# A decoder trunk on one core: a second tile for the queries' low parts, raw output weights in alternating halves of the queries' tile, and three rotating tiles for the heads' outputs

## Chip, core and metric

The kernel runs on one core of one Trainium2 chip. The metric is the device time of one launch in microseconds (us), the median of three runs. Engines are named as in the profile: PE (matrix products, with PEld for the loading of their stationary operand), DVE (elementwise and reductions), ACT (activations and copies), POOL, and SP, whose queue issues most DMAs. Each engine takes its own instructions in the order in which they stand in its queue.

## What is computed

Two layers over 512 tokens of width 1024. Each layer has a mixer (differential attention, a short convolution and gated linear attention, concatenated to width 1024 and projected by `w_out`) and then a PEER block with 16384 single-neuron experts. Cut to the part around the change:

```python
for i in range(2):
    h = rmsnorm(x, norm_mix[i])
    da_q, da_k, da_v, sc_b, sc_c, sc_h, g_q, g_k, g_v, g_r, g_lr = split(h @ w_in[i])
    q, k = rope(da_q), rope(da_k)                    # 4 heads, 2 maps of 64 each
    p = softmax(causal(q @ k.T / 8))                 # for both maps
    o_da = rmsnorm((p[0] - lam * p[1]) @ v) * (1 - lam_init)
    o_sc = sc_b * conv3(sc_c * sc_h)                 # 256 channels
    o_g = rmsnorm(gla(g_q, g_k, g_v, decay)) * silu(g_r)
    x = x + concat(o_da, o_sc, o_g) @ w_out[i]       # 1024 x 1024
    x = x + peer(rmsnorm(x), ...)                    # top-16 of 16384 experts per head
return rmsnorm(x)
```

## The kernel before

Tokens are handled in four blocks of 128 (`tb` 0 to 3). To keep float32 precision on the faster matmul format, an operand is kept as two tiles: `hi`, a rounded copy made by ACT, and `lo`, the difference, made by DVE (`split`, lines 88 to 90). A product is then three matmuls (`mm3`, lines 82 to 86).

**The order of the work.** The program is written as one straight sequence, but a scheduler at build time lays each engine's queue out by readiness, with the program's order as priority, except where `keep_in_program_order` pins an instruction. So work of a later line can stand earlier in a queue, as filler. Tiles are slots of pools: a tile that takes over a slot waits until the last reader of the tile before it is done. Pools are stacked, so a pool that opens after another has closed lies in its space.

**The projections.** `across` and `down` (lines 277 to 295) load 256 columns of `w_in` at a time as a slab, split them and multiply with the normed activations. The result group (`psp`) is gathered in one of two PSUM tiles of `psC`.

**The attention.** The queries stand transposed in `qT`, 128 partitions by 4 heads by 512 tokens, 8 KB in each partition. For a block, `turn_hi` (line 391) makes the tile `qz` with four ACT copies of 64 partitions by 512 elements; `turn_lo` (line 397) makes `ql`, the low part, with two DVE subtractions. There are two tiles `qz0` and `qz1`, taken in turn by the blocks, but one tile `ql` for all blocks, cleared once by POOL (line 388). `attend(tb)` (line 401) goes through `diff_attention` and, per head, `head_weights`: scores on PE (lines 525 to 528), maxima on DVE (529), exponentials on ACT (533), the difference of the two maps on DVE (537), then transposes (553) and products with the values on PE (557). `head_norm` (from line 564) squares on ACT and takes a reciprocal root on DVE by some ten small operations. Blocks 0 and 1 are attended among the convolution's projections; two heads of block 2 are prepared early, at line 432; the rest of block 2 and block 3 follow at line 479, and `turn_lo(3)` stands just ahead of block 3, at line 477, since it can't overwrite `ql` while block 2 reads it.

**The output weights.** `w_out` is eight chunks of 128 rows, taken in the order 6, 7, 4, 5, 0, 1, 2, 3. `load_w` (line 441) fetches one chunk (512 KB) by a DMA from SP's queue into the first half of `qT`, tokens 0 to 255 of each head, whose queries are no longer needed by then; ACT and DVE split it into a tile `wk` of its own. All eight chunks go through this one place, so each fetch waits for the subtraction of the chunk before it. The first three tiles `wk` lie in the keys' tile `kT` and in the pool `early`; the other five in the pool `wout`, which opens when the slabs' pool has closed.

**The output projection.** `head_out` (line 576) transposes a block's heads' outputs and writes them, scaled by `dgain`, to `mh` and `ml`, two tiles for all four blocks. `out_proj(tb)` (line 464) forms two groups (`pso`, 512 columns each) of eight chunks, 24 matmuls a group; DVE adds each to `x`. In the program all four blocks' `head_out` stand ahead of the first `out_proj`. `norm_T` then normalizes block after block for PEER. The last group of block 3 and its addition come in `rest`, pinned among PEER's first instructions: the loads of its query weights into `uraw` (line 781), their splits (784, 785) and the products `psq`.

Of the kernel before, what the change touches and what calls it, by code (L numbers as in the profile page):

```python
# [7 lines left out]
F32 = mybir.dt.float32  # L8
F32R = mybir.dt.float32r
# [5 lines left out]
OP = mybir.AluOpType  # L15
# [4 lines left out]
P = 128  # L20
T = 512
# [51 lines left out]
class K:  # L73
# [156 lines left out]
    def mixer(self, L):  # L230
        nc, tc, ins = self.nc, self.tc, self.ins
        lam_init = 0.8 - 0.6 * math.exp(-0.3 * L)
        right = ExitStack()
        with ExitStack() as mc:
            mp = mc.enter_context(tc.tile_pool(name="mix", bufs=1, reuse_waits="tile"))
            dgain = mp.tile([P, 1], F32, name="dgain")
            cw = mp.tile([P, 2, 3], F32, name="cw")
            qT = mp.tile([P, 4, T], F32, name="qT")
            kT = mp.tile([P, 4, T], F32, name="kT")
            va = mp.tile([P, TB, T], F32, name="va")  # L240
# [6 lines left out]
            with ExitStack() as wc:  # L247
# [29 lines left out]
                def across(c0, n=256):  # L277
                    wh, wl = slab(c0, n)
                    for j in range(n // P):
                        ps = self.psC.tile([P, T], F32, tag="c", name="psp")  # L280
                        for k in range(KD):
                            self.mm3(ps, wh[:, k, j * P:j * P + P], wl[:, k, j * P:j * P + P], hh[:, k], hl[:, k],
                                     k == 0, k == KD - 1)
                        yield j, ps
# [15 lines left out]
                for i, tb in enumerate(ORDER):  # L300
                    if L:
                        ps = self.psv.pop(tb)
                    else:
                        next(norm, None)
                        ps = self.psC.tile([P, 256], F32, tag="c", name="psv")
# [18 lines left out]
                lam = mp.tile([P, 1], F32, name="lam")  # L324
# [4 lines left out]
                for tb in range(TB):  # L329
                    ps = self.psC.tile([P, 272], F32, tag="c", name="psp")  # L330
# [24 lines left out]
                for i in range(4):  # L355
                    dst, h = (qT, kT)[i // 2], i % 2
# [17 lines left out]
                ap = right.enter_context(tc.tile_pool(name="attn", bufs=2, side="right", reuse_waits="tile"))  # L374
                ac = mc.enter_context(ExitStack())
                kp = ac.enter_context(tc.tile_pool(name="early", bufs=1, side="right", reuse_waits="tile"))
                new_w = lambda pool, bufs: pool.tile([P, 2, D], F32R, tag="wk", name="wk", bufs=bufs)
                wk = [new_w(kp, 2) for _ in range(2)]
                kp.tile([P, 40], F32, name="line")
                keys = [kp.tile([P, 4, T], F32R, name=f"ks{m}") for m in range(2)]  # L380
                halves = [slice(64 * m, 64 * m + 64) for m in range(2)]
                for m, r in enumerate(halves):
                    for i in range(0, 4, 2):
                        h = slice(i, i + 2)
                        nc.scalar.copy(keys[m][r, h], kT[r, h])
                        nc.vector.tensor_tensor(keys[m][halves[1 - m], h], kT[r, h], keys[m][r, h].bitcast(F32), op=OP.subtract)
                ql = ap.tile([P, 4, 2, P], F32R, name="ql", bufs=1)
                nc.gpsimd.memset(ql.bitcast(F32), 0.0)
                heads, turned = [], {}

                def turn_hi(tb):
                    qz = turned[tb] = ap.tile([P, 4, 2, P], F32R, tag=f"qz{tb % 2}", name=f"qz{tb % 2}", bufs=1)
                    for m, r in enumerate(halves):
                        for half in halves:
                            nc.scalar.copy(qz[half, :, m], qT[r, :, tb * P:tb * P + P])

                def turn_lo(tb):
                    for m, r in enumerate(halves):
                        nc.vector.tensor_tensor(ql[r, :, m], qT[r, :, tb * P:tb * P + P], turned[tb][r, :, m].bitcast(F32), op=OP.subtract)

                def attend(tb, early=()):
                    heads.append(self.diff_attention(tb, keys, va, (turned[tb], ql), lam, ap, early))

                turn_hi(0)
                turn_lo(0)
                turn_hi(1)
                attend(0)
                z = qp.tile([P, 2, T + 2], F32, tag="z", name="z", bufs=1)
                nc.vector.memset(z[:, :, 0:2], 0.0)
                for j, ps in across(2048):  # L410
                    nc.scalar.copy(z[:, j, 2:], ps)
                turn_lo(1)
                attend(1)
                turn_hi(2)
                turn_lo(2)
                turn_hi(3)
                for j, ps in across(1792):
                    nc.vector.tensor_tensor(z[:, j, 2:], ps, z[:, j, 2:], op=OP.mult)
                nc.sync.dma_start(cw, ins["conv_w"][L])
# [9 lines left out]
                for j, ps in across(1536):  # L429
                    if j == 0:  # L430
                        s0 = self.sums()
                        early = [s0] + [self.head_weights(2, h, keys, (turned[2], ql), lam, ap, s0) for h in range(2)]
                    nc.vector.tensor_tensor(ys[j], ys[j], ps, op=OP.mult)
                    self.split(mch[:, j], mcl[:, j], ys[j])

                korder = (6, 7, 4, 5, 0, 1, 2, 3)
                wo = {}

                by4 = lambda t: t.rearrange("p (a b) -> p a b", a=4)

                def load_w(k, tile, raw):
                    wo[k] = tile
                    nc.sync.dma_start(raw, by4(ins["w_out"][L, k * P:(k + 1) * P, :]))
                    self.split(by4(tile[:, 0]), by4(tile[:, 1]), raw)

                for k, t in zip(korder, [mp.tile([P, 2, D], F32R, tag="kT", name="wk0")] + wk):
                    load_w(k, t, qT[:, :, 0:256])

            with tc.tile_pool(name="wout", bufs=1, reuse_waits="tile") as op_:
                mh = op_.tile([P, 4, T], F32R, name="mh")  # L450
                ml = op_.tile([P, 4, T], F32R, name="ml")
                for k in korder[3:]:
                    load_w(k, new_w(op_, 5), qT[:, :, 0:256])

                def chunk(k, s):
                    if k < 4:
                        return mh[:, k, s], ml[:, k, s]
                    a, b = (mch, mcl) if k < 6 else (mgh, mgl)
                    return a[:, k % 2, s], b[:, k % 2, s]

                def add(xs, ps):
                    return nc.vector.tensor_tensor(xs, xs, ps, op=OP.add)

                def out_proj(tb):
                    for nh in range(2):
                        ps = self.psC.tile([P, T], F32, tag="c", name="pso")
                        n = slice(nh * 512, nh * 512 + 512)
                        for k in korder:
                            self.mm3(ps, *chunk(k, slice(tb * P, tb * P + P)), wo[k][:, 0, n], wo[k][:, 1, n],
                                     k == korder[0], k == korder[-1])  # L470
                        if nh == 0 or tb < TB - 1:
                            add(self.x[:, tb, n], ps)
                    return self.x[:, tb, n], ps

                for tb in range(TB):
                    if tb == 3:
                        turn_lo(3)
                    if tb > 1:
                        attend(tb, early if tb == 2 else ())
                    t = slice(tb * P, tb * P + P)  # L480
                    self.head_out(heads[tb], dgain, mh[:, 0:4, t], ml[:, 0:4, t])
                xh, xl = self.new_act()
                norm = self.norm_T(ins["norm_ffn"][L:L + 1, :], xh, xl,
                                   [ap.tile([P, D], F32, tag=t, name=n, bufs=b) for n, t, b in
                                    (("grow", "qz0", 1), ("sq", "qz1", 1), ("xn0", "e", 2), ("xn1", "e", 2))], self.rs3, rows=self.xrows)
                for tb in range(TB):
                    late = out_proj(tb)
                    if tb < TB - 1:
                        next(norm)

# [927 lines left out]
```

## Time and profile before

| | |
|---|---|
| median of 3 runs | 2873.4 us (2873.01 to 2874.69) |
| the profiled execution, its own time | 2872.77 us |
| its span, first to last instruction | 2870.7 us |
| mean granted PE clock over the span | 0.998 |
| busy over the span | PE 99%, PEld 88%, DVE 86%, ACT 45%, POOL 29% |
| HBM traffic over the span | 273 GB/s |
| output projection of layer 0, first `pso` to first `psq` | 196.2 to 266.4 us |
| output projection of layer 1 | 1619.2 to 1690.0 us |

The profile's times run from the span's start. A line of a timeline gives start, duration, engine, source line, operation, output and inputs, count, and in square brackets how long the engine stood idle before it and whose end released it. A matmul's record is longer than the distance to the next one, because they are pipelined. In tables by stretches of time, each engine's busy microseconds and number of instructions are followed by the mean granted PE clock and the DMA engines' share. SPq is SP's queue, a DMA's issue and not its transfer.

### The profile page before, as it was taken

Reading aid. Unit: us, or ns where it says so; the run is one execution under the profiler, and the core shown is the slowest. Engines: PE = TensorE matmul, PEld = TensorE weight load, DVE = VectorE, ACT = ScalarE, POOL = GpSimd, SP = SyncE. Lnnn points to the kernel's source line nnn. Section 1 sums busy time; section 2 is a strip of 40 time slices with the busy share of each in tenths; the row PEclk is TensorE's granted clock in tenths of the full one; section 3 lists DMA queues with packets and bytes.
Section 4 is the critical chain, followed back from the end, with each engine's and each line's share of the span. In section 5 each row is a group of like instructions: output and inputs, shape, how many; then the busy total and the mean of one; then the engine's idle time right before and its main releaser. Section 6 shows DMA issues by size and latency. Waiting matters only on the chain.

```text
span 2870.7 us, 44994 instructions
## 1 busy us (share of the span) xinstructions
PE 2835.3 (99%) x16328; PEld 2528.3 (88%) x16328; DVE 2468.4 (86%) x4898; ACT 1290.8 (45%) x1946; POOL 840.0 (29%) x713
## 2 busy tenths in 40 slices
PE   8999999999999999999999999999999999999998
PEld 7878899999999988888888788999999999988887
DVE  6685989997998899888966869999979888998888
ACT  6273346675333333333453633556743333333333
POOL 1200002211666565222112000121126655552221
PEclk9999999999999999999999999999999999999999
DMA  4322259998999999999733222699989999999995
GB/s 133 96 71 92 89 164 318 331 307 308 375 383 376 381 377 363 369 359 363 270 99 89 74 85 91 210 314 325 317 303 384 386 379 386 375 363 366 364 357 222
DMA packets 352191, 790.50 MB, mean 275 GB/s; under 512 B 32384, under 2 KB 201248, under 8 KB 347872
## 3 DMA queue, kind: packets, MB, share of 16 engines
q1 hardware_dynamic: 165616, 424.18, 41.1%
q0 software_dynamic: 87136, 312.85, 29.8%
q10 hardware_dynamic: 99216, 50.60, 5.9%
q8 instruction: 128, 2.10, 0.3%
q14 instruction: 95, 0.78, 0.1%
HBM read 705.39 MB, written 78.91 MB: 273 GB/s over the span
## 4 chain that ended last, share of the span: by engine, by line
PE 85%; DVE 9%; ACT 2%; DMA 2%; issue 1%; SPq 0%; DVEq 0%; ACTq 0%
PE pv L85 12%; PE pv L86 12%; PE pv L84 12%; PE psh L84 10%; PE psh L85 10%; PE psh L86 10%; PE psg L1347 2%; PE psq L84 2%; PE psq L85 2%; PE psq L86 2%; PE psp L85 2%; PE psp L86 2%; PE psp L84 2%; DMA qT<-in_w_out 1%; PE pss L819 1%
## 5 line engine op out<-in xcount | busy, mean ns | idle before, releaser
L86 PE MATMUL pv<-vh,wl 128*128 128x512 f32 x1500 | 584.7, 390 | 0.0
L85 PE MATMUL pv<-vl,wh 128*128 128x512 f32 x1500 | 584.6, 390 | 0.0
L84 PE MATMUL pv<-vh,wh 128*128 128x512 f32 x1500 | 583.6, 389 | 0.0
L883 POOL DMA_INDIRECT row<-in_u_rows,idx x256 | 360.2, 1407 | 343.0 <-DVE row L889 225.1
L883 POOL DMA_INDIRECT row<-in_v_rows,idx x256 | 315.6, 1233 | 487.4 <-DVE yacc L896 450.1
L1049 DVE TENSOR_TENSOR vl<-vraw,vh 128x1024 fp32r<-128x1024 f32 x250 | 305.9, 1224 | 91.5 <-issue 79.1
L889 DVE SCALAR_TENSOR_TENSOR row<-row,xg 128x1024 f32<-128x1024 f32 x320 | 382.2, 1218 | 0.1
L1053 ACT CAST vh<-vraw 128x1024 fp32r<-128x1024 f32 x250 | 263.0, 1052 | 194.1 <-PE pv L86 188.0
L1061 ACT CAST wh<-g 128x384 fp32r<-128x384 f32 x250 | 128.4, 513 | 468.1 <-DVE g L1217 458.5
L84 PE MATMUL psh<-ahi,uwb 128*128 128x352 f32 x1024 | 334.1, 326 | 0.0
L84 PE MATMUL psh<-ahi,uwa 128*128 128x352 f32 x1024 | 333.6, 326 | 0.0
L86 PEld LDWEIGHTS pv<-vh,wl 128*128 128x128 f32 x1500 | 281.5, 188 | 58.8
L84 PEld LDWEIGHTS pv<-vh,wh 128*128 128x128 f32 x1500 | 281.6, 188 | 57.5
L85 PEld LDWEIGHTS pv<-vl,wh 128*128 128x128 f32 x1500 | 281.5, 188 | 57.2
L85 PE MATMUL psh<-alo,uwb 128*128 128x352 f32 x1024 | 330.6, 323 | 0.0
L85 PE MATMUL psh<-alo,uwa 128*128 128x352 f32 x1024 | 330.6, 323 | 0.0
L86 PE MATMUL psh<-ahi,uwa 128*128 128x352 f32 x1024 | 327.3, 320 | 0.0
L896 DVE SCALAR_TENSOR_TENSOR yacc<-row,wk,yacc 128x1024 f32<-128x1024 f32 x254 | 325.1, 1280 | 2.0
L86 PE MATMUL psh<-ahi,uwb 128*128 128x352 f32 x1024 | 326.8, 319 | 0.0
L800 ACT ACTIVATE ht<-psh 128x352 f32<-128x352 f32 x256 | 118.9, 465 | 458.7 <-PE psh L86 449.2
L785 DVE TENSOR_TENSOR uwa<-uraw,uwa 128x1024 fp32r<-128x1024 f32 x144 | 175.7, 1222 | 74.2 <-ACT uwa L784 74.0
L785 DVE TENSOR_TENSOR uwb<-uraw,uwb 128x1024 fp32r<-128x1024 f32 x144 | 175.9, 1221 | 57.9 <-ACT uwb L784 57.7
(389 smaller groups left out, 5822.2 us busy)
## 6 DMA issues: line engine op xcount, KB each, us to landing
uraw<-in_peer_u SPq DMA_DIRECT2D x256, 512.0 KB, 5.9
vraw<-in_v_rows SPq DMA_DIRECT2D x252, 512.0 KB, 7.4
G<-stg ACTq DMA_DIRECT2D x48, 1024.0 KB, 7.2
g<-G SPq DMA_DIRECT2D x30, 1536.0 KB, 10.4
H<-ht SPq DMA_DIRECT2D x144, 176.0 KB, 5.3
ht<-H SPq DMA_DIRECT2D x144, 176.0 KB, 8.5
wraw<-in_w_in SPq DMA_DIRECT2D x84, 256.0 KB, 3.2
uraw<-in_peer_w_q SPq DMA_DIRECT2D x32, 512.0 KB, 3.6
```

Source lines behind the costliest of these rows:

```text
L84: mm(ps, ah, bh, start=first, stop=False)
L85: mm(ps, ah, bl, start=False, stop=False)
L86: return mm(ps, al, bh, start=False, stop=last)
L785: self.before, self.last = self.last, pin(nc.vector.tensor_tensor(lo, src, hi.bitcast(F32), op=OP.subtract))
L800: pin(nc.scalar.activation(hs[c][:, 0:TD], ps, AF.Gelu))
L883: nc.gpsimd.indirect_dma_start(out=r, out_offset=None, in_=ins[name], in_offset=bass.IndirectOffsetOnAxis(ap=at, axis=0))
L889: nc.vector.scalar_tensor_tensor(r, r, 1.0, xg, op0=OP.mult, op1=OP.mult, accum_out=out)
L896: nc.vector.scalar_tensor_tensor(acc, r, w, acc, op0=OP.mult, op1=OP.add)
L1049: return pin(nc.vector.tensor_tensor(like(lo, src), src, like(hi.bitcast(F32), src), op=OP.subtract))
L1053: pin(nc.scalar.copy(vh[c], vs[c]))
L1061: pin(nc.scalar.copy(like(wh[c], ws[c]), ws[c]))
L1347: nc.tensor.matmul(ps[:, j], B[at], a[at], start=a is As[0], stop=a is As[-1])
```

## The change

- Two tiles `ql0` and `ql1`, both cleared by POOL at the start; block `tb` uses `ql[tb % 2]`. `turned[tb]` now holds both tiles of a block.
- `turn_lo(1)` moves ahead of `attend(0)`; `turn_lo(3)` moves from the output projection's loop to just behind `turn_hi(3)`, after `attend(1)`.
- `load_w` fetches into the first half of `qT` (tokens 0 to 255) and the second half (256 to 511) in turn.
- `mh` and `ml` (8 KB each in a partition) go. Each block gets a tile `m` of 4 KB for both parts, one of three that rotate; block 3 therefore takes the slot of block 0, and `head_out(3)` moves behind `out_proj(0)`.

```diff
-ql = ap.tile([P, 4, 2, P], F32R, name="ql", bufs=1)
-nc.gpsimd.memset(ql.bitcast(F32), 0.0)
+ql = [ap.tile([P, 4, 2, P], F32R, name=f"ql{i}", bufs=1) for i in range(2)]
+for t in ql:
+    nc.gpsimd.memset(t.bitcast(F32), 0.0)
...
 turn_hi(0)
 turn_lo(0)
 turn_hi(1)
+turn_lo(1)
 attend(0)
...
-turn_lo(1)
 attend(1)
-turn_hi(2)
-turn_lo(2)
-turn_hi(3)
+for tb in (2, 3):
+    turn_hi(tb)
+    turn_lo(tb)
...
-def load_w(k, tile, raw):
+def load_w(k, tile):
+    raw = qT[:, :, 256 * (len(wo) % 2):256 * (len(wo) % 2) + 256]
     wo[k] = tile
     nc.sync.dma_start(raw, by4(ins["w_out"][L, k * P:(k + 1) * P, :]))
     self.split(by4(tile[:, 0]), by4(tile[:, 1]), raw)
...
-mh = op_.tile([P, 4, T], F32R, name="mh")
-ml = op_.tile([P, 4, T], F32R, name="ml")
+ms = {}
 for k in korder[3:]:
-    load_w(k, new_w(op_, 5), qT[:, :, 0:256])
+    load_w(k, new_w(op_, 5))
+
+def hand_over(tb):
+    ms[tb] = op_.tile([P, 2, 4, P], F32R, tag="m", name="m", bufs=3)
+    self.head_out(heads[tb], dgain, ms[tb][:, 0], ms[tb][:, 1])
...
 for tb in range(TB):
-    if tb == 3:
-        turn_lo(3)
     if tb > 1:
         attend(tb, early if tb == 2 else ())
-    t = slice(tb * P, tb * P + P)
-    self.head_out(heads[tb], dgain, mh[:, 0:4, t], ml[:, 0:4, t])
+    if tb < 3:
+        hand_over(tb)
...
 for tb in range(TB):
     late = out_proj(tb)
+    if tb == 0:
+        hand_over(3)
     if tb < TB - 1:
         next(norm)
```

More of the change, by code (lines that the diff above doesn't have):

```diff
@@ L386, in mixer @@
                         nc.vector.tensor_tensor(keys[m][halves[1 - m], h], kT[r, h], keys[m][r, h].bitcast(F32), op=OP.subtract)
-                ql = ap.tile([P, 4, 2, P], F32R, name="ql", bufs=1)
-                nc.gpsimd.memset(ql.bitcast(F32), 0.0)
+                ql = [ap.tile([P, 4, 2, P], F32R, name=f"ql{i}", bufs=1) for i in range(2)]
+                for t in ql:
+                    nc.gpsimd.memset(t.bitcast(F32), 0.0)
                 heads, turned = [], {}
                 def turn_hi(tb):
-                    qz = turned[tb] = ap.tile([P, 4, 2, P], F32R, tag=f"qz{tb % 2}", name=f"qz{tb % 2}", bufs=1)
+                    qz = ap.tile([P, 4, 2, P], F32R, tag=f"qz{tb % 2}", name=f"qz{tb % 2}", bufs=1)
+                    turned[tb] = (qz, ql[tb % 2])
                     for m, r in enumerate(halves):
@@ L398, in turn_lo @@
                     for m, r in enumerate(halves):
-                        nc.vector.tensor_tensor(ql[r, :, m], qT[r, :, tb * P:tb * P + P], turned[tb][r, :, m].bitcast(F32), op=OP.subtract)
+                        nc.vector.tensor_tensor(ql[tb % 2][r, :, m], qT[r, :, tb * P:tb * P + P], turned[tb][0][r, :, m].bitcast(F32), op=OP.subtract)
                 def attend(tb, early=()):
-                    heads.append(self.diff_attention(tb, keys, va, (turned[tb], ql), lam, ap, early))
+                    heads.append(self.diff_attention(tb, keys, va, turned[tb], lam, ap, early))
                 turn_hi(0)
@@ L431, in mixer @@
                         s0 = self.sums()
-                        early = [s0] + [self.head_weights(2, h, keys, (turned[2], ql), lam, ap, s0) for h in range(2)]
+                        early = [s0] + [self.head_weights(2, h, keys, turned[2], lam, ap, s0) for h in range(2)]
                     nc.vector.tensor_tensor(ys[j], ys[j], ps, op=OP.mult)
@@ L446, in mixer, with chunk @@
                 for k, t in zip(korder, [mp.tile([P, 2, D], F32R, tag="kT", name="wk0")] + wk):
-                    load_w(k, t, qT[:, :, 0:256])
+                    load_w(k, t)
             with tc.tile_pool(name="wout", bufs=1, reuse_waits="tile") as op_:
-                mh = op_.tile([P, 4, T], F32R, name="mh")
-                ml = op_.tile([P, 4, T], F32R, name="ml")
+                ms = {}
                 for k in korder[3:]:
-                    load_w(k, new_w(op_, 5), qT[:, :, 0:256])
-                def chunk(k, s):
+                    load_w(k, new_w(op_, 5))
+                def hand_over(tb):
+                    ms[tb] = op_.tile([P, 2, 4, P], F32R, tag="m", name="m", bufs=3)
+                    self.head_out(heads[tb], dgain, ms[tb][:, 0], ms[tb][:, 1])
+                def chunk(k, tb):
                     if k < 4:
-                        return mh[:, k, s], ml[:, k, s]
+                        return ms[tb][:, 0, k], ms[tb][:, 1, k]
                     a, b = (mch, mcl) if k < 6 else (mgh, mgl)
-                    return a[:, k % 2, s], b[:, k % 2, s]
+                    t = slice(tb * P, tb * P + P)
+                    return a[:, k % 2, t], b[:, k % 2, t]
                 def add(xs, ps):
@@ L468, in out_proj @@
                         for k in korder:
-                            self.mm3(ps, *chunk(k, slice(tb * P, tb * P + P)), wo[k][:, 0, n], wo[k][:, 1, n],
+                            self.mm3(ps, *chunk(k, tb), wo[k][:, 0, n], wo[k][:, 1, n],
                                      k == korder[0], k == korder[-1])
```

## The prediction

> **What bounds the kernel now.** I read the page first, for the engine that sets the time; then the chain of waits in the two output projections, for what holds that engine there; then PE's timeline with its idle times, and a table by stretches, for how much it loses.
>
> ```profile
> span 2870.7 us, 44994 instructions
> PE 2835.3 (99%) x16328; PEld 2528.3 (88%) x16328; DVE 2468.4 (86%) x4898; ACT 1290.8 (45%) x1946; POOL 840.0 (29%) x713
> PE 85%; DVE 9%; ACT 2%; DMA 2%; issue 1%; SPq 0%; DVEq 0%; ACTq 0%
> ```
>
> PE is busy for 99% of the span and makes 85% of the chain that ended last. So a microsecond counts where PE stands still, and what PE gains in one stage reaches the end, since the stages behind it hang on PE as well. The 2% of DMA in the chain is the odd entry. The chain of waits, in order of time, shows where it lies (layer 0; start, duration, what):
>
> ```profile
> 206.98 4.57 DMA qT<-in_w_out
> 211.58 1.05 ACT wk L89
> 212.66 1.23 DVE wk L90
> 213.91 3.84 DMA qT<-in_w_out
> 217.77 1.05 ACT wk L89
> 218.85 1.24 DVE wk L90
> 220.10 4.04 DMA qT<-in_w_out
> 224.17 1.05 ACT wk L89
> ```
>
> This is the loop through the one raw place in `qT`: fetch, rounded copy, subtraction, next fetch. From 211.58 to 217.77 is 6.19 us, from there to 224.17 is 6.40 us: one chunk of output weights in 6.3 us. Eight chunks must pass before the first group `pso` can close. What PE loses by it, layer 0 and then layer 1 (PE's timeline; in brackets the idle time before the instruction and its releaser):
>
> ```profile
> 213.94 0.50 PE L85 MATMUL pso<-wk,mh 128*128 128x512 f32 x1 [0.53 <-DVE wk L90]
> 217.14 0.66 PE L581 MATMUL htr<-ident,ho 128*128 128x128 f32 x4 [2.01 <-DVE ho L573]
> 218.87 1.22 PE L84 MATMUL pso<-wk,mh 128*128 128x512 f32 x2 [0.22 <-ACT wk L89]
> 225.26 0.73 PE L84 MATMUL pso<-wk,mh 128*128 128x512 f32 x2 [0.91 <-ACT wk L89]
> ...
> 1623.36 0.50 PE L84 MATMUL pso<-wk,mch 128*128 128x512 f32 x1 [0.80 <-ACT wk L89]
> 1637.64 0.50 PE L85 MATMUL pso<-wk,mh 128*128 128x512 f32 x1 [0.28 <-DVE wk L90]
> 1640.84 0.99 PE L581 MATMUL htr<-ident,ho 128*128 128x128 f32 x4 [1.99 <-DVE ho L573]
> 1648.93 0.73 PE L84 MATMUL pso<-wk,mh 128*128 128x512 f32 x2 [1.01 <-ACT wk L89]
> ```
>
> Six of the eight idle times name the weights. The two of 2 us name `ho`, the heads' output of block 2, but stand behind the same cause: PE had nothing else to do, because the next chunk was not there, and `ho` was late since ACT and DVE take their queues in order and had a weight's copy and subtraction ahead of it, waiting for the DMA. The table by stretches (start:end, length, busy time of PE, PEld, DVE, ACT, POOL, then the granted clock):
>
> ```profile
> 196.00:229.00 33.00, 29.32 (x165) 21.79 (x163) 25.90 (x62) 19.49 (x48) 0.00 (x0) 0.95 0.30 95
> 1619.00:1652.00 33.00, 28.88 (x158) 21.26 (x157) 25.35 (x61) 20.13 (x49) 0.00 (x0) 0.95 0.30 96
> ...
> 150.00:164.00 14.00, 13.68 (x74) 10.58 (x73) 11.78 (x30) 13.62 (x33) 0.00 (x0) 1.00 0.19 58
> 164.00:177.00 13.00, 12.87 (x75) 10.10 (x74) 12.14 (x46) 12.82 (x41) 0.00 (x0) 1.00 0.28 81
> 186.00:196.00 10.00, 10.00 (x57) 8.29 (x55) 9.07 (x20) 5.18 (x13) 0.00 (x0) 1.00 0.19 58
> 240.00:252.00 12.00, 11.95 (x57) 9.59 (x56) 5.08 (x12) 2.23 (x4) 0.00 (x0) 1.00 0.00 0
> ```
>
> PE stands still for 33.00 - 29.32 = 3.68 us and 33.00 - 28.88 = 4.12 us, which is what the eight rows above add up to (3.67 and 4.08). Its clock is 0.95 there and 1.00 in the four stretches below, which costs 0.05 x 33 = 1.65 us in each. Together 5.33 + 5.77 = 11.1 us of 2872.77. The four rows below show PE with work at hand: before 196 the projections' matmuls fill in between the attention's, and from 240 on all eight chunks are there.
>
> **Part 1: the second raw place.** Durations of the loop's pieces over all 16 chunks, in the order minimum/median/maximum in ns, and the DMA's time to landing:
>
> ```profile
> L399 DVE TENSOR_TENSOR ql<-qT,qz x16: 673/687/692, 155.6 to 1625.8; 64x512 fp32r<-64x512 f32 x16
> L89 ACT CAST wk<-qT x16: 1044/1048/1067, 177.3 to 1647.8; 128x1024 fp32r<-128x1024 f32 x16
> L90 DVE TENSOR_TENSOR wk<-qT,wk x16: 1194/1219/1226, 180.0 to 1648.9; 128x1024 fp32r<-128x1024 f32 x16
> DMA to landing us min/median/max: 2.2/3.9/7.9
> ...
> 164.09 0.62 SPq L443 DMA_DIRECT2D qT<-in_w_out  x1
> 181.22 13.70 SPq L443 DMA_DIRECT2D qT<-in_w_out  x3
> 200.59 20.05 SPq L443 DMA_DIRECT2D qT<-in_w_out  x4
> ```
>
> One turn of one place is 3.9 + 1.05 + 1.22 = 6.2 us, as the chain showed. With two places, two turns run side by side: one chunk in 3.1 us, as long as ACT and DVE are there, and they need only 1.05 and 1.22 us for each. The DMA share of 0.30 leaves room for two fetches at once; I take the 3.9 us for both, and the 7.9 of the slowest landing as the other end: then a chunk takes (7.9 + 2.3)/2 = 5.1 us, still less than 6.3.
>
> When can the second half be filled? Its tokens are blocks 2 and 3, so `turn_hi` and `turn_lo` of both must be done. The last four copies of `turn_hi`, and the last matmul of the slabs, whose space the pool `wout` takes over:
>
> ```profile
> 171.56 2.50 ACT L395 CAST qz<-qT 64x512 fp32r<-64x512 f32 x4
> 193.43 0.40 PE L86 MATMUL psp<-ahi,wl 128*128 128x512 f32 x1
> ```
>
> The copies end at 174.1, the two subtractions of `turn_lo(3)` (1.4 us) at about 176: the second chunk's fetch then starts some 5 us ahead of the 181.22 of now, and the third at 181.2, when the first place is free. Six chunks at 3.1 us from 181.2 end at 200; add the 6.2 us of the last turn: 206. If chunks 4 and 5 have to wait for the slabs' end at 193.8, both raw places are full by then and four more chunks at 3.1 us give 206 as well. At 5.1 us a chunk it is 181.2 + 6 x 5.1 + 10.2 = 222. Now the last subtraction ends at 226.5, by the chain: 224.17 + 1.05 + 1.2. At 206 all weights are there before the first idle time of layer 0 (213.4); the only earlier one, layer 1's at 1622.6 (199.6 in layer 0's time), waits for the fourth chunk, which then is there at 194 + 2.3. Both groups of block 0, and then those of block 1, can fill in wherever the attention of block 3 makes PE wait, as the slabs' matmuls did before 196.
>
> The gain is then the 11.1 us less what such a stretch still loses. The rows of 150 to 177 give that: 27.00 - 13.68 - 12.87 = 0.45 us in 27 us, or 0.55 in 33; twice, 1.1 us. So **-10.0 us**.
>
> Both ends of this term. The idle rows don't hold all of the loss: matmul records overlap (57 `pso` and other matmuls of 0.39 us each would be 22 us, and stand in 12 us in the row of 240), so a wait of up to some 0.16 us behind each of the 48 products of block 0 is hidden in busy time. Half of that, 0.08 x 48 = 3.8 us a layer, would make it -18. At the other end only the six waits that name the weights go, 0.53 + 0.22 + 0.91 + 0.80 + 0.28 + 1.01 = 3.75 us, and `ho` stays as late as it is: -3.75.
>
> The Trainium skill, page "Perfetto Trace Analysis", section "Identifying the Most-Contended Engine", holds that matmul busy time hides how far PE is from its limit, and to use the busy share of weight loading. By PEld, with 8.29 of 10 us in the full stretch of 186, the two stretches hold 26.3 and 25.6 us of work: 14.1 us lost, and the time would be 2858.7. My sum keeps to the idle rows and the clock.
>
> **Part 2: `turn_lo` earlier, on DVE.** `turn_lo(1)` goes from behind the first heads' reductions to ahead of them: 2 x 0.69 = 1.4 us ahead of block 0's maxima on DVE, with ACT's exponentials and PE's transposes of block 0 behind. PE has the slabs' matmuls meanwhile (13.68 of 14 us busy), so I cost it at nothing. `turn_lo(3)` is 1.4 us of DVE work taken out of the crowded stretch after 196 and put into 164 to 177, where DVE is busy for 12.14 of 13 us. Again the slabs cover; if they didn't, the two moves cost 2.75 us a layer (a rival, below). What they buy is the free second half. Two `turn_lo` of one parity are now ordered by `qz` alone, whose copies have to wait for the same matmuls as before.
>
> **Part 3: POOL and the tiles `m`.** One more clearing:
>
> ```profile
> L388 POOL MEMSET ql<- x2: 952/957/962, 136.3 to 1559.3; 128x1024 f32 x2
> ```
>
> It ends at 138.3 instead of 137.3, with 17 us to the first use at 155.6 (the row of L399 above): nothing. The writes to `m` have the shapes of those to `mh` and `ml`, and the stationary operand stays 128x128: nothing. Memory: 16 KB of `mh` and `ml` become 12 KB, and `ql` grows from 4 to 8, so no pool has to move further than by 4 KB, and later tiles that take over these places wait for chunks of the last group in place of `mh` and `ml`: from a small loss to a gain below 1 us a layer, taken as nothing.
>
> `head_out(3)` gains a wait: its slot is free when `out_proj(0)` has read block 0's. Behind it in ACT's and DVE's queues stand the norm's copies, and behind those the first load of PEER. The rows now (ACT, DVE, SP, PE):
>
> ```profile
> 234.31 0.69 ACT L582 ACTIVATE mh<-htr,dgain 128x512 fp32r<-128x512 f32 x1 [2.50 <-PE htr L581]
> 227.84 1.28 DVE L462 TENSOR_TENSOR x<-x,pso 128x512 f32<-128x512 f32 x2 [1.28 <-PE pso L86]
> 236.02 0.35 SPq L781 DMA_DIRECT2D uraw<-in_peer_w_q  x1
> 256.95 0.40 PE L84 MATMUL pso<-wk,mh 128*128 128x512 f32 x1
> ```
>
> `out_proj(0)` is added up at 227.84, already 6.5 us before block 3 writes its `mh` at 234.31, and comes earlier with the weights at 206. The first product that needs block 3's `mh` starts at 256.95, 22 us later. So the new wait ends before the old one does: nothing, and it costs only if `out_proj(0)` ended later than now.
>
> **The sum.** 2872.77 - 11.1 + 1.1 = 2862.8 for an execution like the profiled one. The median shown is 0.6 us above it: **2863.4 us**, stated as 2863.
>
> **The rivals.**
>
> *Attention binds, not the weights* (gain small). DVE is busy for 25.90 of 33 us, and `ho` may stay late through its own ten small operations. For: DVE names the two longest waits. Against: PE needs only filler, not `ho`. If no filler stands in PE's queue ahead of those waits, only the named ones go: 2872.77 - 3.75, or 2869.7 by the median.
>
> *The clock stays down.* The 0.95 need not come from these idle times. If it stays, 3.3 us of the gain are gone: 2866.7. Beside it: the Trainium skill, page "TensorE: Matmul & The Clock Gate", Part 1, has the clock halved only after an idle window of about 3.4 us; the longest idle row here is 2.01 us, so by the rule it would be another cause. Against: both drops lie in the two stretches with idle time, and the four other rows have 1.00.
>
> *More than the idle rows* (hidden waits go too): 2872.77 - 18.5, or about 2855.
>
> *Nothing changes.* If ACT's queue holds the copies in an order in which each stands behind the subtraction before it, two places turn no faster than one: 2873.
>
> *DVE binds and it gets slower.* From 150 to 177 DVE and ACT are over 84% busy, and each copy of `qz` and subtraction of `ql` sits ahead of maxima that PE's next scores wait for. If the moved subtractions push the slabs' evacuations on DVE back, PE loses the 2.75 us of Part 2 in each layer, and if the weights then aren't what the attention of block 3 waits for, nothing is won: 2873.4 + 5.5 = 2879. It decides when DVE's free time there, 27.00 - 11.78 - 12.14 = 3.1 us, is used up; the move adds 1.4 us to it. So it needs dependent waits on top, and is unlikely.
>
> **How the numbers follow.** A measurement of this kernel can't tell 0.2%, or 5.7 us, from no change. Forecast (2858 to 2866) 0.58; hidden waits too (below 2858) 0.14; clock stays (2866 to 2868) 0.10; attention binds (2868 to 2871) 0.09; nothing 0.05; slower 0.04. The line at 2867.7 puts the first three on the faster side: 0.82. Attention binds and nothing lie within: 0.14. Slower 0.04. The range from 2854 to 2870 takes in hidden waits and all but the edge of the third case, and leaves out about 0.17.
>
> **What would show it.** Right: SP's issues of `qT<-in_w_out` lie about 3 us apart, two of them at times without a subtraction between; the last subtraction of `wk` near 206 (layer 0); no wait for DMA `qT` in the chain after 200; PE above 32 of 33 us from 196 to 229 with clock 1.00; the first `psq` at about 261 instead of 266.4, and twice that gain in the end. Wrong: PE waits for `ho`, `htr` or `atr` in the place of `wk` (attention); a clock below 1 in a stretch without idle time; PE idle before 196, at `psp` or `pss` (DVE); or a first `psq` that comes 5 us earlier with an end that doesn't.

## The result, and the profile after

The kernel after takes 2858.81 us, the median of six runs (2858.45 to 2859.37); the kernel before takes 2873.44 us, the median of six (2872.79 to 2874.69). The ratio is 0.9949, with a 95% interval of 0.9936 to 0.9962: 14.6 us less. The forecast was 2863, the range 2854 to 2870. The profiled execution of after is the slowest of its six, 2859.37 us; its page begins so, with the chain's shares as the third line:

```profile
span 2857.6 us, 44992 instructions
PE 2831.5 (99%) x16328; PEld 2526.4 (88%) x16328; DVE 2464.9 (86%) x4898; ACT 1292.0 (45%) x1946; POOL 841.6 (29%) x715
PE 89%; DVE 7%; ACT 2%; issue 1%; DMA 1%; DVEq 0%; SPq 0%; ACTq 0%
```

PE's share of the chain has gone from 85 to 89%, DMA's from 2 to 1%. PE's busy time hardly differs (2835.3 before), which shows again that this number doesn't tell where 13 us of span went. The table by stretches does (start:end, length, busy PE, PEld, DVE, ACT, POOL, granted clock, DMA share):

```profile
196.00:229.00 33.00, 32.94 (x183) 25.19 (x182) 23.79 (x59) 19.94 (x49) 0.00 (x0) 1.00 0.20 65
1613.00:1646.00 33.00, 32.93 (x186) 25.44 (x185) 24.22 (x60) 20.33 (x50) 0.00 (x0) 1.00 0.21 65
150.00:164.00 14.00, 13.60 (x74) 10.54 (x73) 12.83 (x32) 13.53 (x30) 0.00 (x0) 1.00 0.43 132
164.00:177.00 13.00, 12.98 (x75) 10.01 (x73) 12.26 (x46) 12.78 (x45) 0.00 (x0) 1.00 0.03 4
```

In both output projections PE stands still for 0.06 and 0.07 us of 33, where it was 3.68 and 4.12, and the clock is 1.00 where it was 0.95. The two rows from 150 to 177 are those to which `turn_lo` was moved: PE's 0.42 us of idle time there stand against 0.45 before. Now the weights' loop in layer 0: SP's issues, ACT's copies and DVE's subtractions (start, duration, what; in brackets the idle time before and its releaser).

```profile
158.82 0.62 SPq L446 DMA_DIRECT2D qT<-in_w_out  x1
175.22 12.22 SPq L446 DMA_DIRECT2D qT<-in_w_out  x4
198.08 6.89 SPq L446 DMA_DIRECT2D qT<-in_w_out  x3
```

```profile
184.56 1.05 ACT L89 CAST wk<-qT 128x1024 fp32r<-128x1024 f32 x1 [2.89 <-DMA qT<-in_w_out]
194.71 1.99 ACT L89 CAST wk<-qT 128x1024 fp32r<-128x1024 f32 x2
202.10 1.05 ACT L89 CAST wk<-qT 128x1024 fp32r<-128x1024 f32 x1 [0.22 <-DMA qT<-in_w_out]
209.04 1.05 ACT L89 CAST wk<-qT 128x1024 fp32r<-128x1024 f32 x1 [0.47 <-DMA qT<-in_w_out]
```

```profile
196.84 2.35 DVE L90 TENSOR_TENSOR wk<-qT,wk 128x1024 fp32r<-128x1024 f32 x2
210.12 1.23 DVE L90 TENSOR_TENSOR wk<-qT,wk 128x1024 fp32r<-128x1024 f32 x1 [0.56 <-ACT wk L89]
```

Chunks 4 and 5 stand in the two places and are copied one behind the other at 194.71, just after the slabs' end (in this trace their last product starts at 193.02 and takes 0.40). The three that are left follow, and the last subtraction ends at 211.35, where it was 226.5. ACT still waits for the DMA in front of some copies, but PE has other products meanwhile: PE's timeline from 193 to 262 names no wait, and the chain has no DMA of `qT` from 177 to 262. In layer 1 the chain still has one, 4.06 us at 1615.49, though PE is busy there too.

PE's timeline also gives the stage its length, from the first product `pso` to the first `psq` of the next stage:

```profile
195.81 0.47 PE L84 MATMUL pso<-wk,mgh 128*128 128x512 f32 x1
...
260.18 0.28 PE L84 MATMUL psq<-ahi,uwa 128*128 128x256 f32 x1
...
1613.23 0.48 PE L84 MATMUL pso<-wk,mgh 128*128 128x512 f32 x1
...
1677.17 0.28 PE L84 MATMUL psq<-ahi,uwa 128*128 128x256 f32 x1
```

So the stages take 64.4 and 63.9 us. Before it was 196.22 to 266.39 and 1619.19 to 1690.01, 70.2 and 70.8. The two stages give 5.8 + 6.9 = 12.7 us of the span's 13.1. The other 0.4 us are there before layer 0's first `pso`: 195.81 instead of 196.22, and already the first matmul `psp` starts at 30.81 instead of 31.55. This is hardly the change's: an experiment below that is as slow as before (the tiles `m` alone) starts `psp` at 30.73. From the end of layer 1's stage to the end of the span it is 1180.4 us, and 1180.7 before, so nothing of the gain is lost behind the stages.

### The profile page after: what moved, and what is told of

It is laid out like the page before. It is cut to its first block, busy times and chain, and to the rows that moved or that the text cites. A ratio compares the mean times of both kernels' runs of the same rounds, so it can differ in the third digit from the quotient of the medians.

```text
span 2857.6 us, 44992 instructions
## 1 busy us (share of the span) xinstructions
PE 2831.5 (99%) x16328; PEld 2526.4 (88%) x16328; DVE 2464.9 (86%) x4898; ACT 1292.0 (45%) x1946; POOL 841.6 (29%) x715
## 4 chain that ended last, share of the span: by engine, by line
PE 89%; DVE 7%; ACT 2%; issue 1%; DMA 1%; DVEq 0%; SPq 0%; ACTq 0%
PE pv L85 12%; PE pv L86 12%; PE pv L84 12%; PE psh L84 10%; PE psh L85 10%; PE psh L86 10%; PE psp L86 2%; PE psp L85 2%; PE psp L84 2%; PE psg L1354 2%; PE psq L84 2%; PE psq L85 2%; PE psq L86 2%; PE pss L826 1%; PE pso L84 1%
```

## The experiments

The theory: the second raw place takes PE's waits for output weights away, and the clock's loss with them; the other edits cost and gain nothing. The rivals: the earlier `turn_lo` or the rotation of `m` make part of the gain; or a shorter turn makes it, and two whole chunks at once aren't needed. Stage lengths are those of one profiled execution each, times are medians.

| kernel | us (lowest to highest, runs) | ratio to before, 95% | layer 0 | layer 1 |
|---|---|---|---|---|
| before | 2873.65 and 2873.69 on the two chips | 1 | 70.2 | 70.8 |
| after | 2858.81 (2858.45 to 2859.37, 6) | 0.9949 [0.9936, 0.9962] | 64.4 | 63.9 |
| one place | 2871.28 (2870.40 to 2872.39, 11) | 0.9993 [0.9984, 1.0002] | 69.7 | 69.4 |
| `m` only | 2873.84 (2872.31 to 2874.59, 11) | 0.9999 [0.9990, 1.0008] | 72.0 | 71.0 |
| two quarters | 2863.84 (2862.79 to 2865.70, 5) | 0.9964 [0.9950, 0.9978] | 65.7 | 66.8 |
| four quarters | 2862.43 (2862.01 to 2862.92, 5) | 0.9961 [0.9947, 0.9974] | 65.7 | 65.3 |
| layer 0 only | 2865.57 (2864.71 to 2865.99, 7) | 0.9971 [0.9960, 0.9982] | 64.3 | 69.7 |
| hand-over after 1 | 2859.89 (2858.88 to 2861.58, 5) | 0.9952 [0.9938, 0.9965] | 64.0 | 64.2 |
| hand-over after 2 | 2860.90 (2859.37 to 2861.33, 5) | 0.9953 [0.9940, 0.9967] | 64.7 | 64.4 |

**One place.** All of the change but the alternation:

```
-raw = qT[:, :, 256 * (len(wo) % 2):256 * (len(wo) % 2) + 256]
+raw = qT[:, :, 0:256]
```

> The changed kernel with its second raw place taken away: every chunk of output weights goes through tokens 0 to 255 of qT again; two ql tiles, the earlier turn_lo and the three tiles m stay. Theory (the single raw place starves PE of weights): all of the gain goes, 2873 us within 3, chunks again 6.3 us apart, PE idle again 3 to 4 us of the 33 us after the first pso in each layer. Rival A (the gain comes from turn_lo(3) leaving the crowded stretch, from the tiles m, or from the memory they free): most of the gain stays, 2859 to 2863. Rival B (any edit reorders the queues, and this order happened to be a good one): anywhere between, with weights still on time.

Measured: 2.4 us less than before, with an interval that takes in no difference, and 12.5 us more than after. PE's waits are back, and the copies of the chunks lie 6.2 to 6.8 us apart again from 184.56 on (table by stretches, then three of the five waits of PE's timeline in layer 0):

```profile
196.00:229.00 33.00, 28.38 (x165) 21.43 (x164) 24.74 (x60) 20.07 (x52) 0.00 (x0) 1.00 0.26 84
1619.00:1652.00 33.00, 29.96 (x166) 22.73 (x165) 24.20 (x59) 20.48 (x54) 0.00 (x0) 0.95 0.25 80
```

```profile
216.31 0.63 PE L588 MATMUL htr<-ident,ho 128*128 128x128 f32 x4 [1.87 <-DVE ho L580]
217.64 0.73 PE L84 MATMUL pso<-wk,m 128*128 128x512 f32 x2 [0.27 <-ACT wk L89]
224.22 0.74 PE L84 MATMUL pso<-wk,m 128*128 128x512 f32 x2 [1.60 <-ACT wk L89]
```

So 12.5 of the 14.6 us hang on the alternation; the interval leaves open whether the other edits bring anything. The stretches lose 33.00 - 28.38 = 4.62 us in layer 0 with the clock at 1.00, and 3.04 + 0.05 x 33 = 4.69 us in layer 1 with the clock at 0.95: nearly the same loss with and without the slow clock. That matters for the clock rival, below.

**The tiles `m` alone.** The kernel before with the rotation and the hand-over only:

```
-mh = op_.tile([P, 4, T], F32R, name="mh")
-ml = op_.tile([P, 4, T], F32R, name="ml")
+ms = {}
...
+def hand_over(tb):
+    ms[tb] = op_.tile([P, 2, 4, P], F32R, tag="m", name="m", bufs=3)
+    self.head_out(heads[tb], dgain, ms[tb][:, 0], ms[tb][:, 1])
```

> The kernel before with only the three rotating tiles m and head_out(3) behind out_proj(0); one ql, one raw place. Theory: nothing, 2873.4 within 2; head_out(3) ends when it did, since out_proj(0) was done 6 us before it. Rival A: 2 to 14 us faster through the freed memory, or slower by some us through the new wait. With the run of one raw place it gives the price of ql and turn_lo by difference: 0 to 3 us by the theory.

Measured: no difference within 0.1%. The stages are not shorter (72.0 and 71.0), so the tiles `m` gain nothing by themselves.

**Two quarters.** The kernel before, with nothing changed but the fetch: each chunk comes as two halves of 256 KB, and the halves take turns in the two quarters of the same first half of `qT`.

```
-nc.sync.dma_start(raw, by4(ins["w_out"][L, k * P:(k + 1) * P, :]))
-self.split(by4(tile[:, 0]), by4(tile[:, 1]), raw)
+for i in range(2):
+    c = slice(i * 512, i * 512 + 512)
+    raw = qT[:, :, i * P:i * P + P]
+    nc.sync.dma_start(raw, by4(ins["w_out"][L, k * P:(k + 1) * P, c]))
+    self.split(by4(tile[:, 0, c]), by4(tile[:, 1, c]), raw)
```

> The kernel before with two raw places and nothing else: each chunk is fetched as two half chunks of 256 KB into tokens 0 to 127 and 128 to 255 of qT, which are free where the one place was. No second ql, no moved turn_lo, no m. Twice as many DMAs, copies and subtractions of half the size. Theory: most of the gain is there without the rest of the change: a chunk takes one turn of half size, about 3 + 0.6 + 0.7 = 4.3 us in place of 6.3, the last subtraction comes 12 to 14 us earlier, 2859 to 2864. Rival A: 2870 to 2876, as nothing of what it names is there. Rival B: no forecast.

Measured: 9.8 us less, two thirds of the change's gain, without `ql`, `m` or `turn_lo` being touched, at the upper edge of what was expected. The last subtraction of layer 0 starts at 216.06 and takes 0.69, so it ends 9.8 us earlier than before, less than the 12 to 14 expected. What is needed is that fetch, copy and subtraction of different pieces overlap; the room for it was there already. Of the 5.0 us that are missing to after, 4.2 lie in the stages, 65.7 and 66.8 against 64.4 and 63.9.

**Four quarters.** After, with half chunks through all four quarters:

```
-nc.sync.dma_start(raw, by4(ins["w_out"][L, k * P:(k + 1) * P, :]))
-self.split(by4(tile[:, 0]), by4(tile[:, 1]), raw)
+q = 2 * (len(wo) % 2)
+for i in range(2):
+    c = slice(i * 512, i * 512 + 512)
+    raw = qT[:, :, (q + i) * P:(q + i) * P + P]
+    nc.sync.dma_start(raw, by4(ins["w_out"][L, k * P:(k + 1) * P, c]))
+    self.split(by4(tile[:, 0, c]), by4(tile[:, 1, c]), raw)
```

> The changed kernel with four raw places: half chunks go through all four quarters of qT in turn. Theory: after the change PE has no idle time left in the output projections (0.06 of 33 us), so faster weights bring nothing: 2859 within 2, though the weights arrive earlier. If weights still bound PE unseen, 2 to 4 us faster. If 32 DMAs, copies and subtractions in place of 16 cost ACT and DVE time that counts, 1 to 3 us slower.

Measured: 2862.43 us, 3.6 more than after. The 2859 of the theory was missed; the sign is that of the other case, more instructions that cost time, and the size is a little above its 1 to 3 us. The weights are there sooner (the last copy of layer 0 starts at 206.99 instead of 209.04), and yet the stages are 1.3 and 1.4 us longer. PE's timeline has one wait of this size in each that after doesn't have:

```profile
201.65 0.49 PE L84 MATMUL pso<-wk,m 128*128 128x512 f32 x1 [0.88 <-ACT wk L89]
...
1620.40 0.50 PE L84 MATMUL pso<-wk,m 128*128 128x512 f32 x1 [0.87 <-ACT wk L89]
```

The wait names the sixth chunk, but that chunk isn't late: its first copy ends at 201.60, and in after its copy ends at 203.15. What PE lacks is other work. ACT's rows with four quarters, then in after:

```profile
200.98 0.62 ACT L89 CAST wk<-qT 128x512 fp32r<-128x512 f32 x1 [2.96 <-DMA qT<-in_w_out]
201.50 0.47 ACT L565 COPY aT<-atr 128x384 f32<-128x384 f32 x1
```

```profile
200.83 0.48 ACT L562 COPY aT<-atr 128x384 f32<-128x384 f32 x1 [2.97 <-PE atr L560]
```

With four quarters the sixth chunk's copy stands ahead of the attention's copy `aT` in ACT's queue and waits for its DMA until 200.98. The transposes that `aT` copies end at 200.31, but `aT` starts at 201.50, and PE's products `po` that read it at 202.22. In after `aT` stands ahead of the sixth chunk's copy (202.10), starts as soon as its transposes are done, and `po` fills PE from 201.36 on. Layer 1 shows the same order, with the copy at 1619.73 and `aT` at 1620.26. This is read from the two traces; no run changes the order of ACT's queue alone.

The groups of copies and subtractions from 177 to 262 (busy us, mean ns) also cost more, here and then in after:

```profile
L90 DVE TENSOR_TENSOR wk<-qT,wk 128x512 fp32r<-128x512 f32 x16 | 10.5, 684 | 1.4 <-ACT wk L89 1.3
L89 ACT CAST wk<-qT 128x512 fp32r<-128x512 f32 x16 | 9.3, 622 | 5.9 <-DMA qT<-in_w_out 5.8
```

```profile
L90 DVE TENSOR_TENSOR wk<-qT,wk 128x1024 fp32r<-128x1024 f32 x8 | 9.7, 1222 | 2.8 <-ACT wk L89 2.8
L89 ACT CAST wk<-qT 128x1024 fp32r<-128x1024 f32 x8 | 8.3, 1049 | 3.6 <-DMA qT<-in_w_out 3.6
```

A half costs 684 and 622 ns, not half of 1222 and 1049. So an earlier last chunk isn't worth anything by itself; what counts is that PE finds work at any point. The other 0.9 us of the 3.6 aren't in these stages, and their cause is open.

**Layer 0 only.** After, with the alternation in the first layer only:

```
+raw = qT[:, :, 256 * (len(wo) % 2):256 * (len(wo) % 2) + 256] if L == 0 else qT[:, :, 0:256]
```

> The changed kernel with the second raw place in layer 0 alone; layer 1 uses the one place. Theory: layers add up, so 5.8 us of stage gain from layer 0 stays and 6.8 of layer 1 goes: 2873.4 - 6.5 = 2867 within 2. Rival A: no dependence on the raw places, 2859 to 2863. Rival B: not additive, anywhere from 2859 to 2874.

Measured: 8.1 us less than before, 6.8 more than after. Layer 0's stage is that of after, layer 1's that of one place (the table by stretches, layer 0 and layer 1):

```profile
196.00:229.00 33.00, 32.93 (x185) 25.16 (x182) 23.93 (x60) 20.08 (x49) 0.00 (x0) 1.00 0.20 65
1613.00:1646.00 33.00, 28.61 (x166) 21.35 (x165) 25.34 (x60) 20.02 (x49) 0.00 (x0) 1.00 0.28 89
```

So the gain comes stage by stage: layer 0's stage is 5.9 us shorter than before, the alternation in layer 1 brings another 5.8 there (69.7 against 63.9), and both reach the end undiminished.

**Hand-over later.** After, with block 3's heads handed over behind `out_proj(1)`, and in another kernel behind `out_proj(2)`, instead of `out_proj(0)`:

```
-if tb == 0:
+if tb == 1:
     hand_over(3)
```

> The changed kernel with head_out(3) moved one block later, behind out_proj(1). Theory: block 3's tile is first read in the last but one pair of groups, so head_out(3) still has some 10 us: no change, 2859 within 2. Rival (head_out(3) is near a limit, through the load of uraw that waits for it or through DVE's order): 3 us slower or more.

> The changed kernel with head_out(3) behind out_proj(2), directly ahead of its reader. Theory: now transposes, copy and subtraction (0.6 + 0.7 + 0.75 us) and the first uraw load stand right before the groups that need them; the k order reads block 3's tile only at the fifth chunk, 2.8 us into the group, so it costs 0 to 3 us a layer: 2859 to 2865. If it costs more, the first uraw load (held by dgain) delays psq: up to 5 us a layer, 2869.

Measured: 1.1 and 2.1 us more than after, taken on different chips; the intervals of the ratios overlap almost wholly. The stages themselves stay at 64.0 to 64.7. With the hand-over behind `out_proj(1)` PE shows one new wait behind each stage, among the products `psq` (PE's timeline):

```profile
269.08 1.07 PE L218 MATMUL psn<-ident,xn 128*128 128x128 f32 x8 [1.05 <-DVE xn L212]
...
1687.91 1.06 PE L218 MATMUL psn<-ident,xn 128*128 128x128 f32 x8 [1.40 <-DVE xn L212]
```

Behind `out_proj(2)` only layer 1 has such a wait, of 1.00 us. So the place that the change chose has room for a delay as far as the weights' products go. Whether the later hand-over causes the waits in the norm wasn't tested.

## Why the prediction was right, step by step

**The term of the second place was right in cause and somewhat small.** It took 11.1 us (idle rows and clock of two stretches) less 1.1 us that such a stretch would still lose. The residual was mis-sized: 0.06 + 0.07 = 0.13 us was left, with products of `pso` to fill in, less than the slabs' matmuls left from 150 to 177. That is 1.0 us. The rest of the difference between 10.0 and 12.7 us, 1.7 us, lies outside the prediction's idle rows and clock: some 0.5 us in layer 0 (5.8 + 0.06 - 5.33) and 1.2 us in layer 1 (6.9 + 0.07 - 5.77). About 0.5 of it is idle time that the prediction's table left out: from 229 us, and in layer 1 from 1652 us, to the end of the stage PE stood still for 0.33 and 0.35 us before, and in after, from 229 and 1646 us, for 0.08 in each. The other 1.2 us, 0.3 and 0.9, neither the idle rows nor the clock show. The prediction had priced such loss, hidden in overlapping matmul records, at 3.8 us a layer; that this is what it was isn't shown.

The measured 14.6 us are 4.6 more than the forecast: the 1.0, the 1.7, the 0.4 ahead of the stages, and 1.5 by which the medians lie further apart than the two profiled spans. The last two belong to no step of the prediction. 2858.81 lies inside the case that was forecast, but only 0.8 us from its edge.

The Trainium skill, page "Perfetto Trace Analysis", section "Identifying the Most-Contended Engine", gave 14.1 us by the busy share of weight loading. The trace bears that measure out better than the prediction's own sum: its time for an execution like the profiled one, 2858.7, was measured as 2859.37, though the stages gained 12.7 and not 14.1. PEld did rise in the two stretches, from 21.79 and 21.26 us to 25.19 and 25.44. As full as the stretch from 186 on (8.29 of 10 us) it would be 27.4 of 33, so by this measure PE still has 7 to 8% to spare there.

**The time of the last weights was wrong by 5 us, at no cost.** It was put at 206 and is 211.35. The step that failed is that both places come free when the slabs end. Chunks 4 and 5 were copied at 194.71 as said, but their subtractions started at 196.84 and ran one behind the other for 2.35 us, so the next fetch could start only at 198.08, 4.7 us behind the slabs' end (193.02 + 0.40). The forecast held because PE's demand for the last chunks is later still.

**`turn_lo`, `ql`, POOL and `m` at nothing** were right within what can be measured: the tiles `m` alone change the time by 0.2 us, all but the alternation by -2.4 us, with an interval that takes in no change. The stages with one place are 0.5 and 1.4 us shorter than before in one execution each, which would fit `turn_lo(3)` leaving the crowded stretch. Whether it is that isn't shown.

**`head_out(3)`'s new wait** cost nothing, though the step came later, against the wording that it ends before the old one does. ACT, DVE and SP:

```profile
236.73 0.69 ACT L589 ACTIVATE m<-htr,dgain 128x512 fp32r<-128x512 f32 x1 [0.23 <-PE htr L588]
237.46 0.75 DVE L590 SCALAR_TENSOR_TENSOR m<-htr,dgain,m 128x512 fp32r<-128x512 f32 x1
238.23 0.35 SPq L788 DMA_DIRECT2D uraw<-in_peer_w_q  x1
```

ACT's write is 2.4 us later than the 234.31 of before, and SP's first load of PEER 2.2 us later than 236.02, while the whole stage ends 6.2 us sooner. Nothing waits for it: `psq` starts at once behind the last `pso`.

**The rivals.** That attention binds falls with the first stretch: no wait for `ho` is left, so `ho` was late because of the weights, as argued; with one place PE waits for it again, 1.87 us in layer 0. That nothing changes falls with one place against after. That DVE binds falls with the rows from 150 to 177. Hidden waits was at most a small case: 1.2 us that the rows don't show, and not the 7.6 it was priced at. The clock rival fell too, since the stretches of after have a clock of 1.00. On its price the runs say something that the prediction didn't have: with one place layer 0 lost 4.62 us at full clock, and layer 1 4.69 us with 1.65 us of it as clock. With the alternation in layer 0 only, layer 1 works as with one place; it had no slow step, lost 4.39 us to idle time alone, and its stage took 69.7 us against 69.4. So where PE waits for weights anyway, a slow step costs nothing that these three stages show: PE works longer and waits less. The two terms may be added up in one stretch, but the clock's is no separate gain there. What a slow step costs with work at hand, the rival's 3.3 us, no run shows.

## What to carry to other kernels

A loop of fetch, copy and subtraction through one place runs at the sum of its steps, here 6.3 us a chunk, however idle each engine is. Where PE waits for that loop, give it a second place, even by cutting the one in two, and PE gets back its idle time and its slow clock of that stretch. Take both from the one row of the stretch, and check them against the stage's length rather than against the engine's busy time over the span. Don't take sooner for faster: pieces of half the size had the last weights ready sooner, and the kernel was 3.6 us slower. Look at what stands behind a copy that waits for its DMA in its engine's queue.

## What the runs showed of the clock

The slow clock comes in steps of one length, and doesn't need PE to be idle throughout. In the traces' record of the clock, the granted clock of before is 0.50 from 217.60 to 221.02 and from 1640.96 to 1644.37, 3.413 us each, and so it is in one place (1639.53 to 1642.95) and in `m` only (219.82 to 223.24, 1643.18 to 1646.59). The two starts lie 1423.36 us apart in before and in `m` only alike, which is 417 times 3.4133. The stretches at full clock, from one change to the next, are whole numbers of the same step, in all nine traces: 58, 416 and 358 steps in before (197.97, 1419.94 and 1221.97 us), 830 in after (2833.06 us). So in these runs the clock changes on a fixed grid. The stretches of the grid ahead of the slow one, then the slow one, in before, in one place, and in `m` only (behind the length: PE's busy time):

```profile
214.19:217.60 3.41, 1.40 (x8) 0.91 (x8) 2.53 (x12) 0.00 (x0) 0.00 (x0) 1.00 0.50 154
217.60:221.01 3.41, 3.19 (x13) 2.23 (x12) 1.89 (x2) 3.24 (x6) 0.00 (x0) 0.50 0.00 0
1637.55:1640.96 3.41, 1.33 (x5) 0.82 (x6) 2.87 (x14) 0.00 (x0) 0.00 (x0) 1.00 0.47 153
```

```profile
1636.12:1639.53 3.41, 1.49 (x10) 1.06 (x9) 2.36 (x11) 0.34 (x1) 0.00 (x0) 1.00 0.50 154
...
212.76:216.17 3.41, 1.68 (x8) 1.02 (x6) 3.17 (x13) 0.00 (x0) 0.00 (x0) 1.00 0.51 154
216.17:219.59 3.42, 2.68 (x17) 2.04 (x18) 1.89 (x2) 3.04 (x6) 0.00 (x0) 1.00 0.00 0
```

```profile
213.00:216.41 3.41, 1.91 (x6) 0.93 (x6) 3.17 (x13) 0.62 (x4) 0.00 (x0) 1.00 0.20 43
216.41:219.82 3.41, 1.62 (x10) 1.16 (x10) 1.41 (x3) 1.65 (x3) 0.00 (x0) 1.00 0.32 111
219.82:223.24 3.42, 3.12 (x14) 2.91 (x14) 2.44 (x5) 1.81 (x5) 0.00 (x0) 0.50 0.30 103
...
1639.77:1643.18 3.41, 1.06 (x8) 0.86 (x8) 1.60 (x7) 0.73 (x1) 0.00 (x0) 1.00 0.46 154
```

Where PE was busy for 1.06 to 1.62 of 3.41 us, the clock was halved for the next 3.41; at 1.68 and 1.91 it was not, with 212.76 found by going back 1423.36 us from the start of the slow stretch in layer 1 of the same run. The whole grid says the same. From the first full clock to the last, the nine traces hold 7489 such steps. In 14 of them PE was busy for at most 1.62 us, these five and the last one of each trace, and half clock followed each time; in all others PE was busy for at least 1.68 us, and full clock followed each time. So the line lies between 1.62 and 1.68 of 3.41 us, a little under half, with the caution that the ends of busy times are modelled.

This also answers a doubt in the prediction. The Trainium skill, page "TensorE: Matmul & The Clock Gate", Part 1, speaks of an idle window of about 3.4 us. The length agrees, but a step of 3.41 us with idle times of at most 2.01 us in it was enough, so these waits were the cause of the slow clock after all.
